# Latent and context convolved by one instruction per tap, and six heads' k and v handed to the delta rule's preparation in on-chip tiles

## Chip, core and metric

The kernel runs on one core of one Trainium2 chip. TensorE multiplies matrices, VectorE, ScalarE and GpSimd do the elementwise work, and SyncE (SP) issues the DMAs. The metric is the device time of one execution in microseconds (us), lower is better.

## The reference, cut to what matters

The program is a three-layer sequence model on 512 latent positions (8 rows of 64) and 256 context positions, width 2048. The change lies in the first layer. There the input is projected by `w_in`, and the projections go through a convolution over 5 neighbouring positions and a silu. In the latent part the convolution runs within rows of 64, in the context along all 256:

```python
xbc_l = jax.nn.silu(conv_latent(xbc_l, conv_ssd_w) + conv_ssd_b)
xbc_c = jax.nn.silu(centred_dwconv(xbc_c, conv_ssd_w) + conv_ssd_b)
qkv_l = jax.nn.silu(conv_latent(qkv_l, conv_gdn_w))
qkv_c = jax.nn.silu(centred_dwconv(qkv_c, conv_gdn_w))
ssd_c, ssd_l = ssd_mixer(xbc_c, dt_c, xbc_l, dt_l, ssd_a_log, ssd_dt_bias, ssd_d)
gdn_c, gdn_l = gdn_mixer(qkv_c, b_c, a_c, qkv_l, b_l, a_l, gdn_a_log, gdn_dt_bias)
```

`ssd_mixer` is a state-space scan over chunks of 128 positions in both directions. `gdn_mixer` is the delta rule: for each of 8 heads k is normalized, k kT of each chunk is decayed and masked, a unit lower triangular system is solved per chunk, and a scan in both directions follows. The two later layers use none of this.

## The kernel before, in words

Phase A of layer 1 works in channel-major form. One *block* is 128 output channels: a *gemm* accumulates `mm` (128 channels x 512 latent positions) and `mmc` (128 x 256 context positions) in PSUM over 16 slices of the width, with three products each, since weights and activations are split in a high part (`wh`, `hi`) and a low one (`wl`, `xlo`). L200 is the line of these products, L185 and L186 split the weights. Four PSUM buffers (pool `pm`) hold `mm` and `mmc`, so two blocks are in flight.

When a block's products are done, `conv5` convolves it. ScalarE copies PSUM into a padded tile (L438) and writes the middle tap, scaled (L440, with a bias L442); VectorE adds four more taps (L444); ScalarE takes a tanh (L446) and VectorE multiplies (L447), which together make the silu, as the taps are halved beforehand. Context (`cvc`) and latent part (`cvl`) each go through this on their own. 26 blocks have both parts, and four latent ones (two C blocks, q0, q1) have one.

Then a *sink* uses the result. For the SSD these are `xt`, `Bf`/`Bt` and `Cf`, read by `ssd_unit` (units 0 to 3, four heads each). A unit first runs backward (d=1): per chunk, state products `st`, the state `H` (L620, L622), the product `yo` of the state with C (L603), and `y` (L607). Then forward (d=0), where `ssd_diag` adds the part within a chunk: `Rf`/`Rb` (rows of the decay, by DMA), `Z` (L649), Z times exp (L652), `yd` (L655), and y's sum (L658 to L663). At the end `yT` transposes y, ScalarE copies it to `yf` (L629) and a DMA stores it to `yr`. For the delta rule, k and v of each head are stored to DRAM, `kD` and `vD` (L800, L801), and `gdn_prep(h)` loads them back as `kf` and `vf` (L670, L672), makes the decay E, transposes k and v, and stores ktD, vtD, ED, XD, LX. `gdn_solve` solves two heads' systems at a time, on GpSimd.

Heads 0 and 1's k and v are convolved between units 1 and 2, those of heads 2 to 7 between the preparations: k2, preparation 0, v2, preparation 1, k3, preparation 2, v3, and so on. The pool of the SSD units (`sp`) is released after unit 3, and the preparations' pool (`gp`) is opened on the same side of the memory, over it:

```python
            self.ssd_unit(u, self.xts[u])
        self.sp.release()
        self.b2 = tc.alloc_tile_pool(name="b2", bufs=1, side="right")
        with tc.tile_pool(name="gp", bufs=1, side="right") as self.gp:
            self.gemm([bk(2)])
            self.gdn_prep(0)
            self.gemm([bv(2)])
            self.gdn_prep(1)
```

The engines' queues in phase A are not in the order of the source. The framework's scheduler orders the whole block when the kernel is built, from its own estimates, and the pools limit what may be moved: a gemm's block stands where a PSUM tile is free by its reckoning. In before the gemms of k2 to v3 stand among unit 3's products. After phase A come q1 and the first gate block z0, and phase B, the scan with the other gate blocks z1 and on woven into it.

Of the kernel before, what the change touches and what calls it, by code (L numbers as in the profile page):

```python
# [9 lines left out]
F32 = mybir.dt.float32  # L10
F32R = mybir.dt.float32r
AF = mybir.ActivationFunctionType
# [3 lines left out]
P = 128  # L16
# [5 lines left out]
MUL, ADD, SUB, MAX, MIN = ALU.mult, ALU.add, ALU.subtract, ALU.max, ALU.min  # L22
# [111 lines left out]
class Prog:  # L134
# [278 lines left out]
        return self.hc[:, o:o + 1]  # L413

    def pads_lat(self, pool):
        self.pads(pool, 0)

    def pads(self, pool, nctx=2):
        nc = self.nc
        self.padl = [pool.tile([P, 8, 68], F32, name=f"padl{i}") for i in range(2)]  # L420
        self.padc = [pool.tile([P, 1, 260], F32, name=f"padc{i}") for i in range(nctx)]
        for p, n in [(p, 64) for p in self.padl] + [(p, 256) for p in self.padc]:
            nc.gpsimd.memset(p[:, :, 0:2], 0.0)
            nc.gpsimd.memset(p[:, :, n + 2:n + 4], 0.0)
        self.npl = self.npc = 0

    def conv5(self, ps, is_lat, taps, bias, out, th):

        nc = self.nc
        if is_lat:  # L430
            pad, n, r = self.padl[self.npl % len(self.padl)], 64, 8
            self.npl += 1
        else:
            pad, n, r = self.padc[self.npc % len(self.padc)], 256, 1
            self.npc += 1
        pv = ps.rearrange("p (r n) -> p r n", r=r)
        ov = out.rearrange("p (r n) -> p r n", r=r)
        nc.scalar.activation(out=pad[:, :, 2:n + 2], in_=pv, func=AF.Copy)  # L438
        if bias is None:
            nc.scalar.activation(out=out, in_=ps, func=AF.Identity, scale=taps[2])  # L440
        else:
            nc.scalar.activation(out=out, in_=ps, func=AF.Identity, scale=taps[2], bias=bias)  # L442
        for j in (0, 1, 3, 4):
            nc.vector.scalar_tensor_tensor(out=ov, in0=pad[:, :, j:j + n], scalar=taps[j], in1=ov,  # L444
                                           op0=MUL, op1=ADD)
        nc.scalar.activation(out=th, in_=out, func=AF.Tanh)  # L446
        nc.vector.scalar_tensor_tensor(out=out, in0=th, scalar=1.0, in1=out, op0=ADD, op1=MUL)  # L447

    def both(self, src, done, share=None):

# [7 lines left out]
                    acts=[(self.xh, self.xl, ps[:m, :], "l%d" % id(ps)),  # L458
                          (self.ch, self.cl, pc[:m, o:o + 256], "c%d" % id(pc))], done=done)

    def conv_block(self, names, j, has_bias, sink):

        taps = [self.h(names + str(i), j) for i in range(5)]
        bias = self.h("cb", j) if has_bias else None

        def done(ps, pc=None):
            outs = []
            for p, n, t in ((pc, 256, "c"), (ps, 512, "l")):
                if p is None:
                    outs.append(None)  # L470
                    continue
                o = self.cv.tile([P, n], F32, tag="cv" + t, name="cv" + t)
                th = self.cv.tile([P, 512], F32, tag="cth", name="cth", bufs=1)
                self.conv5(p, t == "l", taps, bias, o, th[:, :n])
                outs.append(o)
            sink(outs[1], outs[0])
        return done

    def small_done(self, ps, pc):
# [186 lines left out]
    def gdn_prep(self, h):  # L666
        nc, g = self.nc, self.gp
        v6 = lambda a: a.rearrange("p (c n) -> p c n", n=P)
        kf = g.tile([P, 768], F32, name="kf")
        nc.sync.dma_start(kf, self.kD[h])  # L670
        vf = g.tile([P, 768], F32, name="vf")
        nc.sync.dma_start(vf, self.vD[h])  # L672
        E = g.tile([P, 768], F32, name="E")
        Rb = g.tile([P, 768], F32, name="Rgb")
        nc.sync.dma_start(E, self.AA[64 + h].partition_broadcast(P))
# [1 line left out]
        for c in range(6):  # L677
            s = slice(c * P, (c + 1) * P)
# [14 lines left out]
        junk = g.tile([P, P], F32, name="junk", bufs=1)  # L693
        for c0, n in ((0, 4), (4, 2)):
            q = self.sc("kT")
            self.transposes(q, None, [kf[:, (c0 + i) * P:(c0 + i + 1) * P] for i in range(n)])
# [9 lines left out]
        for d in range(2):  # L706
            nc.vector.tensor_tensor(out=self.Dg[:, h, d], in0=self.beg[:, :, 8 * d + h], in1=rk2, op=MUL)
            nc.vector.tensor_tensor(out=self.DDE[:, h, d], in0=self.Dg[:, h, d],
                                    in1=self.DEg[:, :, 8 * d + h], op=MUL)

        vt = g.tile([P, 6, P], F32, name="vt")
        for c0, n in ((0, 4), (4, 2)):
            q = self.sc("vT")
            self.transposes(q, None, [vf[:, (c0 + i) * P:(c0 + i + 1) * P] for i in range(n)])
            nc.vector.tensor_tensor(out=vt[:, c0:c0 + n], in0=v6(q[:, :n * P]),
                                    in1=ss[:, c0:c0 + n].unsqueeze(2).to_broadcast([P, n, P]), op=MUL)
        nc.sync.dma_start(self.vtD[h], vt)
        masked(1, vf[:, 0:512], nc.gpsimd, self.mL)

        X = g.tile([P, 768], F32, name="X")  # L720
        for c0, n in ((0, 4), (4, 2)):
            q = self.sc("kk")
            for i in range(n):
                s = slice((c0 + i) * P, (c0 + i + 1) * P)
                nc.tensor.matmul(q[:, i * P:(i + 1) * P], kf[:, s], kf[:, s], start=True, stop=True)
# [6 lines left out]
        for b in range(4):  # L732
            r = slice(32 * b, 32 * b + 32)
# [34 lines left out]
    def phase_a(self):  # L768
        nc, tc, D = self.nc, self.tc, self.D
# [17 lines left out]
        self.xts = {}  # L787

        def sink_x(j):
            def f(lat, ctx):  # L790
# [78 lines left out]

    def query_conv(self, h, ps):  # L870
        o = self.b2.tile([P, 512], F32, name="qf", bufs=2)
        th = self.cv.tile([P, 512], F32, tag="cth", name="cth", bufs=1)
        self.conv5(ps, True, [self.h(f"cg{i}", h) for i in range(5)], None, o, th)
        self.qf.append(o)


# [1169 lines left out]
```

## Time and profile before

| | before |
|---|---|
| median of 3 runs | 3466.33 us (3462.2 to 3469.05) |
| profiled execution | 3458.53 us, span 3456.8 us |
| mean granted TensorE clock | 0.99 |
| TensorE busy | 3342.1 us (97%) |
| VectorE busy | 2084.7 us (60%) |
| ScalarE busy | 1448.1 us (42%) |
| GpSimd busy | 416.3 us (12%) |
| DMA | 482.04 MB, 139 GB/s over the span |

Busy shares are means over the whole span; phase A takes about a fifth of it, 0 to some 710 us, and the stretches in it are told apart by the windows. The clock is a share of full speed, 1.0 for 2.4 GHz and 0.5 for 1.2 GHz. The profiled execution is 7.8 us below the median of the runs.

### The profile page before, as it was taken

The page shows a single profiled execution, that of the slowest core. Times are in us where ns is not written, and L with a number is a line of the kernel's source. Part 1 is how long each engine was busy: PE and PEld are TensorE (multiplying, and loading weights), DVE is VectorE, ACT ScalarE, POOL GpSimd, SP SyncE. Part 2 cuts the span into 40 slices and gives each one's busy share as a digit, 9 for nine tenths or more (in the row PEclk, how much of TensorE's full clock was granted, in tenths as well). Part 3 has the DMA queues.
Part 4 walks back from the last instruction along what each step waited for, and adds up shares of the span by engine and source line. Part 5 has one row for each costly group of instructions (what it writes and reads, how often), then busy time and mean ns, then how long its engine had stood idle before and what let it go on. Part 6 is the DMA issues. An engine that isn't in the chain of part 4 may idle for free.

```text
span 3456.8 us, 47795 instructions
## 1 busy us (share of the span) xinstructions
PE 3342.1 (97%) x16950; PEld 2786.7 (81%) x16950; DVE 2084.7 (60%) x4117; ACT 1448.1 (42%) x2923; POOL 416.3 (12%) x596
## 2 busy tenths in 40 slices
PE   5999999899999999999999999999999999999998
PEld 4888888778888787778888788887888888878887
DVE  5678768778765647776747644555444444353456
ACT  4343335354444336664434444343333333342334
POOL 0011127821110000002313100000000000000000
PEclk8999999999999999999999999999999999999999
DMA  9533338555443854433333744543333333354345
GB/s 375 188 101 103 86 115 255 171 165 156 125 119 99 283 194 161 112 110 101 107 96 97 224 133 126 155 119 109 106 104 104 102 100 103 95 159 128 89 130 172
DMA packets 278350, 482.04 MB, mean 139 GB/s; under 512 B 51976, under 2 KB 85128, under 8 KB 273888
## 3 DMA queue, kind: packets, MB, share of 16 engines
q1 hardware_dynamic: 278112, 479.00, 46.8%
q8 instruction: 133, 2.18, 0.3%
q14 instruction: 105, 0.86, 0.1%
HBM read 417.53 MB, written 61.34 MB: 139 GB/s over the span
## 4 chain that ended last, share of the span: by engine, by line
PE 76%; DVE 9%; DMA 8%; POOL 2%; ACT 2%; issue 2%; SPq 0%; DVEq 0%; ACTq 0%; POOLq 0%
PE mm L200 57%; PE mm L228 3%; PE mm L230 3%; PE mm L232 3%; PE mmc L200 2%; DVE wl L186 2%; PE pl L200 1%; PE mg L930 1%; DMA Rf<-AA 1%; DMA araw<-yF 1%; PE pr L349 1%; DMA wa<-in_wada 1%; PE s L200 1%; DMA E<-AA 1%; POOL E L679 1%
## 5 line engine op out<-in xcount | busy, mean ns | idle before, releaser
L200 PE MATMUL mm<-hi,wl 128*128 128x512 f32 (+2 forms) x3632 | 1416.0, 391 | 15.9 <-DVE wl L186 10.3
L200 PE MATMUL mm<-xlo,wh 128*128 128x512 f32 (+2 forms) x3632 | 1420.8, 391 | 0.2
L200 PE MATMUL mm<-hi,wh 128*128 128x512 f32 (+2 forms) x3632 | 1414.9, 390 | 0.0
L186 DVE TENSOR_TENSOR wl<-wr,wh 128x512 fp32r<-128x512 f32 (+1 forms) x940 | 653.2, 700 | 647.8 <-ACT wh L185 644.9
L185 ACT ACTIVATE wh<-wr 128x512 fp32r<-128x512 f32 (+1 forms) x940 | 580.4, 621 | 1080.4 <-PE mm L200 860.3
L200 PEld LDWEIGHTS mm<-hi,wl 128*128 128x128 f32 (+1 forms) x3632 | 685.1, 189 | 141.6 <-DVE wl L186 14.8
L200 PEld LDWEIGHTS mm<-xlo,wh 128*128 128x128 f32 (+1 forms) x3632 | 685.1, 189 | 135.8 <-issue 2.9
L200 PEld LDWEIGHTS mm<-hi,wh 128*128 128x128 f32 (+1 forms) x3632 | 684.9, 189 | 120.0 <-issue 4.3
L232 PE MATMUL mm<-wh,hi 128*128 128x512 f32 x384 | 150.4, 392 | 0.0
L230 PE MATMUL mm<-wh,xlo 128*128 128x512 f32 x384 | 149.7, 390 | 0.0
L228 PE MATMUL mm<-wl,hi 128*128 128x512 f32 x384 | 149.7, 390 | 0.0
L223 DVE TENSOR_TENSOR wl<-wr,wh 128x512 fp32r<-128x512 f32 x96 | 69.7, 727 | 94.1 <-ACT wh L222 93.8
L222 ACT ACTIVATE wh<-wr 128x512 fp32r<-128x512 f32 x96 | 60.6, 631 | 152.3 <-PE mm L232 95.5
L200 PE MATMUL mmc<-xlo,wh 128*128 128x256 f32 x368 | 106.1, 288 | 0.0
L444 DVE SCALAR_TENSOR_TENSOR cvl<-padl,hc,cvl 128x512 f32<-128x512 f32 x112 | 90.2, 812 | 25.7 <-ACT cvl L440 15.6
L200 PE MATMUL mmc<-hi,wl 128*128 128x256 f32 x368 | 105.6, 287 | 0.0
L200 PE MATMUL mmc<-hi,wh 128*128 128x256 f32 x368 | 105.5, 287 | 0.0
L228 PEld LDWEIGHTS mm<-wl,hi 128*128 128x128 f32 x384 | 72.1, 188 | 15.0 <-DVE pad L1360 0.3
L230 PEld LDWEIGHTS mm<-wh,xlo 128*128 128x128 f32 x384 | 72.1, 188 | 15.0
L232 PEld LDWEIGHTS mm<-wh,hi 128*128 128x128 f32 x384 | 72.1, 188 | 14.5
L200 PEld LDWEIGHTS mmc<-xlo,wh 128*128 128x128 f32 x368 | 70.0, 190 | 15.7
L200 PEld LDWEIGHTS mmc<-hi,wh 128*128 128x128 f32 x368 | 69.9, 190 | 15.1
(585 smaller groups left out, 3992.2 us busy)
## 6 DMA issues: line engine op xcount, KB each, us to landing
wr<-in_o_in SPq DMA_DIRECT2D x192, 256.0 KB, 3.1
wr<-in_e_in SPq DMA_DIRECT2D x160, 256.0 KB, 3.1
wr<-in_pgate SPq DMA_DIRECT2D x148, 256.0 KB, 3.4
wa<-in_wada SPq DMA_DIRECT2D x16, 2048.0 KB, 10.4
wr<-in_w_qkv SPq DMA_DIRECT2D x96, 256.0 KB, 3.4
wr<-in_w_z SPq DMA_DIRECT2D x64, 256.0 KB, 3.2
wr<-in_w_out SPq DMA_DIRECT2D x64, 256.0 KB, 3.7
wg<-in_wgate SPq DMA_DIRECT2D x16, 1024.0 KB, 7.2
```

Source lines behind the costliest of these rows:

```text
L185: nc.scalar.activation(out=hi, in_=r, func=AF.Copy)
L186: nc.vector.tensor_tensor(out=lo, in0=r, in1=hi.bitcast(F32), op=SUB)
L200: nc.tensor.matmul(ap, w[:, kk, :], x, start=(n == 0), stop=(n == total[key] - 1))
L222: nc.scalar.activation(out=hi, in_=r, func=AF.Copy)
L223: nc.vector.tensor_tensor(out=lo, in0=r, in1=hi.bitcast(F32), op=SUB)
L228: nc.tensor.matmul(ps[c][:, :n], self.xh[k][:, t], lo[:, i], start=first, stop=False)
L230: nc.tensor.matmul(ps[c][:, :n], self.xl[k][:, t], hi[:, i], start=False, stop=False)
L232: nc.tensor.matmul(ps[c][:, :n], self.xh[k][:, t], hi[:, i], start=False, stop=last)
L349: nc.tensor.matmul(pr[32 * j:32 * j + 32, 0:256], c32[:, 4 * q + j, :], w[:, 4 * q + j, :], start=(q == 0), stop=(q == 3), tile_position=( ...
L444: nc.vector.scalar_tensor_tensor(out=ov, in0=pad[:, :, j:j + n], scalar=taps[j], in1=ov, op0=MUL, op1=ADD)
L679: nc.gpsimd.tensor_scalar(out=E[:, s], in0=E[:, s], scalar1=self.AAg[:, c, h:h + 1], scalar2=None, op0=SUB)
L930: nc.tensor.matmul(v[:, c], lhs[:, c], rhs[:, c], start=True, stop=True)
```

## The change

`conv5` takes both parts at once. One padded tile of 12 rows x 68 holds the 8 latent rows and the context as 4 rows of 64, whose margins hold the neighbouring context values; two copies of 3 rows x 66 out of PSUM, at offsets 0 and 62, fill these rows with their margins. Each tap, the tanh and the final multiply are then one instruction on 768 columns. The tanh is written into the padded tile, and the tile `cth` is gone. The results lie in one tile of 768, latent first.

For heads 2 to 7 this tile is a `kv` tile of the pool `gp`, of which there are six, and `gdn_prep` reads k and v from it. Their v is no longer stored to DRAM, k still is (the scan loads it later). Heads 0 and 1 are stored and loaded as before, with two loads each. GpSimd's masked E, which was written over vf, has a tile of its own, `Em`.

```diff
     def pads_lat(self, pool):
-        self.pads(pool, 0)
-
-    def pads(self, pool, nctx=2):
+        self.pads(pool, 8)
+
+    def pads(self, pool, rows=12):
         nc = self.nc
-        self.padl = [pool.tile([P, 8, 68], F32, name=f"padl{i}") for i in range(2)]
-        self.padc = [pool.tile([P, 1, 260], F32, name=f"padc{i}") for i in range(nctx)]
...
+        self.pad = [pool.tile([P, rows, 68], F32, name=f"pad{i}") for i in range(2)]
...
-    def conv5(self, ps, is_lat, taps, bias, out, th):
+    def conv5(self, ps, pc, taps, bias, out):
...
-        nc.scalar.activation(out=pad[:, :, 2:n + 2], in_=pv, func=AF.Copy)
-        if bias is None:
-            nc.scalar.activation(out=out, in_=ps, func=AF.Identity, scale=taps[2])
...
+        nc.scalar.activation(out=pad[:, 0:8, 2:66], in_=ps.rearrange("p (r n) -> p r n", r=8), func=AF.Copy)
+        parts = [(ps, out[:, 0:512])]
+        rows = 8
+        if pc is not None:
+            rows = 12
+
+            w = lambda o: bass.AP(tensor=pc.tensor, offset=pc.offset + o, ap=[list(pc.ap[0]), [64, 3], [1, 66]])
+            nc.scalar.activation(out=pad[:, 8:11, 2:68], in_=w(0), func=AF.Copy)
+            nc.scalar.activation(out=pad[:, 9:12, 0:66], in_=w(62), func=AF.Copy)
+            parts.append((pc, out[:, 512:768]))
+        for p, o in parts:
+            if bias is None:
+                nc.scalar.activation(out=o, in_=p, func=AF.Identity, scale=taps[2])
...
+        ov = out.rearrange("p (r n) -> p r n", r=rows)
         for j in (0, 1, 3, 4):
-            nc.vector.scalar_tensor_tensor(out=ov, in0=pad[:, :, j:j + n], scalar=taps[j], in1=ov,
+            nc.vector.scalar_tensor_tensor(out=ov, in0=pad[:, 0:rows, j:j + 64], scalar=taps[j], in1=ov,
                                            op0=MUL, op1=ADD)
-        nc.scalar.activation(out=th, in_=out, func=AF.Tanh)
-        nc.vector.scalar_tensor_tensor(out=out, in0=th, scalar=1.0, in1=out, op0=ADD, op1=MUL)
+
+        th = pad[:, 0:rows, 2:66]
+        nc.scalar.activation(out=th, in_=ov, func=AF.Tanh)
+        nc.vector.scalar_tensor_tensor(out=ov, in0=th, scalar=1.0, in1=ov, op0=ADD, op1=MUL)
...
-    def conv_block(self, names, j, has_bias, sink):
+    def conv_block(self, names, j, has_bias, sink, keep=False):
...
+            n = 512 if pc is None else 768
+            o = (self.gp.tile([P, 768], F32, tag="kv", name="kv", bufs=6) if keep else
+                 self.cv.tile([P, 768], F32, tag="cv", name="cv"))[:, :n]
+            self.conv5(ps, pc, taps, bias, o)
+            sink(o[:, 0:512], None if pc is None else o[:, 512:768])
...
     def gdn_prep(self, h):
-        kf = g.tile([P, 768], F32, name="kf")
-        nc.sync.dma_start(kf, self.kD[h])
-        vf = g.tile([P, 768], F32, name="vf")
-        nc.sync.dma_start(vf, self.vD[h])
+        def chunks(dst):
+            lat, ctx = self.kv.pop((id(dst), h), (None, None))
+            if lat is None:
+                t = g.tile([P, 768], F32, tag="kv", name="kv", bufs=6)
+                lat, ctx = t[:, 0:512], t[:, 512:768]
+                nc.sync.dma_start(lat, dst[h, :, 256:768])
+                nc.sync.dma_start(ctx, dst[h, :, 0:256])
+            return [ctx[:, 0:P], ctx[:, P:2 * P]] + [lat[:, c * P:(c + 1) * P] for c in range(4)]
+
+        kf, vf = chunks(self.kD), chunks(self.vD)
...
-        masked(1, vf[:, 0:512], nc.gpsimd, self.mL)
+        masked(1, g.tile([P, 512], F32, name="Em"), nc.gpsimd, self.mL)
...
         def sink_kv(dst, h):
             def f(lat, ctx):
-                nc.sync.dma_start(dst[h, :, 256:768], lat)
-                nc.sync.dma_start(dst[h, :, 0:256], ctx)
+                if h > 1:
+                    self.kv[id(dst), h] = lat, ctx
+                if h < 2 or dst is self.kD:
+                    nc.sync.dma_start(dst[h, :, 256:768], lat)
+                    nc.sync.dma_start(dst[h, :, 0:256], ctx)
             return f
...
-        bk = lambda h: self.both(K(h), cb("cg", 8 + h, False, sink_kv(self.kD, h)))
-        bv = lambda h: self.both(V(h), cb("cg", 16 + h, False, sink_kv(self.vD, h)))
+        bk = lambda h: self.both(K(h), cb("cg", 8 + h, False, sink_kv(self.kD, h), h > 1))
+        bv = lambda h: self.both(V(h), cb("cg", 16 + h, False, sink_kv(self.vD, h), h > 1))
```

Lines behind conv5 have other numbers in the changed kernel: L446 is the scaled copy there (L440 before), L607 and L619 are yo and st (L603 and L615), L633 is yf (L629), L659 is yd (L655).

In the order of TensorE before, this is the place where k3 (mm_5012, mmc_5013) ends and v3 (mm_5246, mmc_5247) begins; yo, yd and st are unit 3's.

```order
L200 MATMUL mm_5012<-hi_910,wh_5106 128x512
L200 MATMUL mmc_5013<-xlo_918,wh_5106 128x256
L200 MATMUL mmc_5013<-hi_917,wh_5106 128x256
L200 MATMUL mm_5246<-hi_295,wl_5251 128x512
L603 MATMUL yo_4283<-H_4280,Cf_3353 128x256
L655 MATMUL yd_4308<-xt_4058,Z_4289 128x64 x4
L615 MATMUL st_4322<-xd_4320,Bt_3259 128x256
L200 MATMUL mmc_5247<-hi_302,wl_5251 128x256
L200 MATMUL mm_5246<-xlo_296,wh_5250 128x512
```

In the changed kernel TensorE's order has this at the end of v2 (mm_4586, mmc_4587):

```order
L200 MATMUL mm_4586<-hi_910,wh_4680 128x512
L200 MATMUL mmc_4587<-xlo_918,wh_4680 128x256
L200 MATMUL mmc_4587<-hi_917,wh_4680 128x256
L619 MATMUL st_4114<-xd_4112,Bt_3174 128x256
L607 MATMUL yo_4119<-H_4116,Cf_3267 128x256
L619 MATMUL st_4124<-xd_4122,Bt_3174 128x256
L607 MATMUL yo_4129<-H_4126,Cf_3267 128x256
L619 MATMUL st_4134<-xd_4132,Bt_3174 128x256
L607 MATMUL yo_4139<-H_4136,Cf_3267 128x256
L619 MATMUL st_4144<-xd_4142,Bt_3174 128x256
```

and this at the end of unit 3, 15 rows on, where k3 (mm_4882) begins:

```order
L619 MATMUL st_4292<-xd_4290,Bt_3174 128x256
L607 MATMUL yo_4297<-H_4294,Cf_3267 128x256
L659 MATMUL yd_4322<-xt_3948,Z_4303 128x64 x4
L314 MATMUL yT_4334<-ident_78,y_4103 128x128 x3
L314 MATMUL yT_4342<-ident_78,y_4103 128x128 x3
L314 MATMUL yT_4334<-ident_78,y_4103 128x128
L314 MATMUL yT_4342<-ident_78,y_4103 128x128
L200 MATMUL mm_4882<-hi_295,wl_4887 128x512
L200 MATMUL mm_4882<-xlo_296,wh_4886 128x512
```

Between v2's last product and k3's first there are 25 rows, all of unit 3; before, gemm products stand among them.

ScalarE in the changed kernel, at the end of unit 3: `kv_4479` is k2's tile and `kv_4708` that of v2, both written from their PSUM tiles.

```order
L650 ACTIVATE Z_4303<-cbL_3270,dts_1482 128x128 x4
L633 ACTIVATE yf_4339<-yT_4334 128x512
L633 ACTIVATE yf_4347<-yT_4342 128x512
L446 ACTIVATE kv_4479<-mm_4357,hc_93 128x512
L446 ACTIVATE kv_4479<-mmc_4358,hc_93 128x256
L446 ACTIVATE kv_4708<-mm_4586,hc_93 128x512
L446 ACTIVATE kv_4708<-mmc_4587,hc_93 128x256
L455 ACTIVATE pad0_928<-kv_4479 128x12x64
```

The scaled copies of k2 and v2 stand behind both yf copies; before, the scaled copies of k2, v2 and k3 stand ahead of these.

SP's queue before, at the preparation of head 7 (`vD_942`, `ktD_944` and so on are its stores), up to the branch that ends phase A's block:

```order
L801 DMA vD_942<-cvc_6949 128x256
L800 DMA vD_942<-cvl_6959 128x512
L672 DMA vf_7056<-vD_942 128x768
L701 DMA ktD_944<-kt_7077 128x768
L766 DMA LT_948<-T_5768 96x1024
L717 DMA vtD_945<-vt_7105 128x768
L687 DMA ED_943<-vf_7056 128x512
L728 DMA XD_946<-X_7119 128x768
```

and the same place in the changed kernel:

```order
L700 DMA ED_939<-Rgb_6819 128x512
L700 DMA ED_939<-Em_6877 128x512
L182 DMA wr_7024<-in_w_z 128x512
L182 DMA wr_7042<-in_w_z 128x512
L714 DMA ktD_940<-kt_6837 128x768
L730 DMA vtD_941<-vt_6865 128x768
L740 DMA XD_942<-X_6880 128x768
```

The store and load of v7 are gone, and both masked E are stored ahead of ktD.

## Rows read from the trace of the kernel before

**Rows 1.** Windows: stretch, length, busy PE PEld DVE ACT POOL, clock, DMA, GB/s
```profile
148.00:441.00 293.00, 289.06 (x1670) 252.65 (x1669) 235.96 (x544) 128.69 (x284) 37.92 (x46) 1.00 0.37 99
441.00:449.00 8.00, 4.58 (x15) 3.70 (x14) 6.59 (x12) 1.72 (x4) 3.12 (x4) 0.67 0.41 114
449.00:703.00 254.00, 238.04 (x1365) 207.58 (x1363) 189.05 (x372) 107.87 (x292) 156.98 (x226) 0.98 0.61 188
703.00:760.00 57.00, 50.31 (x248) 42.03 (x247) 40.57 (x90) 25.28 (x54) 9.24 (x12) 0.91 0.60 173
```

**Rows 2.** Waits of PE, 520 to 700: total us, times, longest
```profile
PE vT L314 <- DMA vf<-vD: 10.5, 4, 5.3
PE kT L314 <- DVE Xs L738: 2.7, 1, 2.7
PE vT L314 <- DVE cvl L444: 1.7, 1, 1.7
PE kT L314 <- DMA kf<-kD: 1.0, 1, 1.0
```

**Rows 3.** Instructions of source line L444: ns min/median/max
```profile
L444 DVE SCALAR_TENSOR_TENSOR cvl<-padl,hc,cvl x112: 734/745/1300, 147.3 to 676.2; 128x512 f32<-128x512 f32 x112
L444 DVE SCALAR_TENSOR_TENSOR cvc<-padc,hc,cvc x104: 440/477/1896, 151.8 to 678.8; 128x256 f32<-128x256 f32 x104
```

**Rows 4.** Lines by form, ACT, 140 to 720: busy us, mean ns
```profile
L438 ACT ACTIVATE padc<-mmc 128x256 f32<-128x256 f32 x23 | 8.8, 383 | 0.0
```

**Rows 5.** Timeline of DVE, and between them the chain, 426 to 448
```profile
427.24 0.41 DVE L663 TENSOR_TENSOR y<-yt,yd 128x256 f32<-128x256 f32 x1
...
431.08 4.92 DMA Rf<-AA
...
444.49 0.42 DVE L622 TENSOR_TENSOR H<-H,st 128x256 f32<-128x256 f32 x1
```

**Rows 6.** Timeline of PE and DVE, one backward step: start us, us
```profile
458.62 0.59 PE L603 MATMUL yo<-H,Cf 128*128 128x256 f32 x2
...
459.26 0.42 DVE L607 TENSOR_TENSOR y<-yo,EAs 128x256 f32<-128x256 f32 x1 [1.28 <-PE yo L603]
459.69 0.42 DVE L622 TENSOR_TENSOR H<-H,st 128x256 f32<-128x256 f32 x1
```

**Rows 7.** Lines by form, DVE, 140 to 720: busy us, mean ns
```profile
L649 DVE SCALAR_TENSOR_TENSOR Z<-cbU,dts,Z 128x128 f32<-128x128 f32 x64 | 22.3, 384 | 0.0
...
L652 DVE TENSOR_TENSOR Z<-Z,Rf 128x512 f32<-128x512 f32 x16 | 10.8, 680 | 0.0
```

**Rows 8.** Chain that ended last, 480 to 512: start us, us, what
```profile
484.22 0.43 PE yo L603 x2
484.65 0.84 PE yd L655 x8
...
495.89 0.61 ACT yf L629
496.51 3.44 DMA yr<-yf
...
500.66 2.16 DMA yr<-yf
```

**Rows 9.** Windows of two stretches, columns as in Rows 1
```profile
25.00:50.00 25.00, 9.95 (x78) 5.54 (x79) 16.30 (x26) 15.04 (x29) 0.00 (x0) 0.61 1.01 391
441.00:444.50 3.50, 0.64 (x4) 0.38 (x2) 3.40 (x6) 0.56 (x2) 2.51 (x3) 0.88 0.42 128
444.50:449.00 4.50, 3.94 (x11) 3.32 (x12) 3.19 (x7) 1.16 (x3) 0.62 (x1) 0.50 0.41 104
```

**Rows 10.** Timeline of SP, and tile vf's transfers: us to landing
```profile
682.34 0.33 SPq L800 DMA_DIRECT2D vD<-cvl  x1
...
698.56 2.59 SPq L182 DMA_DIRECT2D wr<-in_w_z  x4
...
DMA to landing us min/median/max: 2.0/3.3/6.8
```

More of the change, by code (lines that the diff above doesn't have):

```diff
@@ L415, in pads_lat @@
     def pads_lat(self, pool):
-        self.pads(pool, 0)
-    def pads(self, pool, nctx=2):
+        self.pads(pool, 8)
+    def pads(self, pool, rows=12):
         nc = self.nc
-        self.padl = [pool.tile([P, 8, 68], F32, name=f"padl{i}") for i in range(2)]
-        self.padc = [pool.tile([P, 1, 260], F32, name=f"padc{i}") for i in range(nctx)]
[L422 to L425, printed above, removed]
@@ L427, in conv5 @@
-    def conv5(self, ps, is_lat, taps, bias, out, th):
-        nc = self.nc
[L430 to L437, printed above, removed]
-        nc.scalar.activation(out=pad[:, :, 2:n + 2], in_=pv, func=AF.Copy)
-        if bias is None:
-            nc.scalar.activation(out=out, in_=ps, func=AF.Identity, scale=taps[2])
-        else:
-            nc.scalar.activation(out=out, in_=ps, func=AF.Identity, scale=taps[2], bias=bias)
+        self.pad = [pool.tile([P, rows, 68], F32, name=f"pad{i}") for i in range(2)]
@@ new lines, in pads @@
+        for p in self.pad:
+            nc.gpsimd.memset(p[:, 0:min(rows, 9), 0:2], 0.0)
+            nc.gpsimd.memset(p[:, 0:8, 66:68], 0.0)
+            if rows > 8:
+                nc.gpsimd.memset(p[:, 11, 66:68], 0.0)
+        self.np = 0
+    def conv5(self, ps, pc, taps, bias, out):
+        nc = self.nc
+        pad = self.pad[self.np % 2]
+        self.np += 1
+        nc.scalar.activation(out=pad[:, 0:8, 2:66], in_=ps.rearrange("p (r n) -> p r n", r=8), func=AF.Copy)
[10 more added lines that the diff above has]
+                nc.scalar.activation(out=o, in_=p, func=AF.Identity, scale=taps[2])
+            else:
+                nc.scalar.activation(out=o, in_=p, func=AF.Identity, scale=taps[2], bias=bias)
+        ov = out.rearrange("p (r n) -> p r n", r=rows)
@@ L466, in done @@
         def done(ps, pc=None):
[L467 to L476, printed above, removed]
+            n = 512 if pc is None else 768
[3 more added lines that the diff above has]
+            sink(o[:, 0:512], None if pc is None else o[:, 512:768])
         return done
@@ L668, in gdn_prep @@
         v6 = lambda a: a.rearrange("p (c n) -> p c n", n=P)
-        kf = g.tile([P, 768], F32, name="kf")
-        nc.sync.dma_start(kf, self.kD[h])
-        vf = g.tile([P, 768], F32, name="vf")
-        nc.sync.dma_start(vf, self.vD[h])
+        nc, g = self.nc, self.gp
+        v6 = lambda a: a.rearrange("p (c n) -> p c n", n=P)
+        def chunks(dst):
[7 more added lines that the diff above has]
+        kf, vf = chunks(self.kD), chunks(self.vD)
         E = g.tile([P, 768], F32, name="E")
@@ L695, in gdn_prep @@
             q = self.sc("kT")
-            self.transposes(q, None, [kf[:, (c0 + i) * P:(c0 + i + 1) * P] for i in range(n)])
+            self.transposes(q, None, kf[c0:c0 + n])
             nc.scalar.activation(out=kt[:, c0:c0 + n], in_=v6(q[:, :n * P]), func=AF.Copy)
@@ L713, in gdn_prep @@
             q = self.sc("vT")
-            self.transposes(q, None, [vf[:, (c0 + i) * P:(c0 + i + 1) * P] for i in range(n)])
+            self.transposes(q, None, vf[c0:c0 + n])
             nc.vector.tensor_tensor(out=vt[:, c0:c0 + n], in0=v6(q[:, :n * P]),
@@ L723, in gdn_prep @@
             for i in range(n):
-                s = slice((c0 + i) * P, (c0 + i + 1) * P)
-                nc.tensor.matmul(q[:, i * P:(i + 1) * P], kf[:, s], kf[:, s], start=True, stop=True)
+                nc.tensor.matmul(q[:, i * P:(i + 1) * P], kf[c0 + i], kf[c0 + i], start=True, stop=True)
             nc.vector.tensor_tensor(out=X[:, c0 * P:(c0 + n) * P], in0=q[:, :n * P],
@@ L786, in phase_a @@
         K, V = (lambda h: D["w_qkv"][8 + h]), (lambda h: D["w_qkv"][16 + h])
-        self.xts = {}
+        self.xts, self.kv = {}, {}
         def sink_x(j):
@@ L871, in query_conv @@
         o = self.b2.tile([P, 512], F32, name="qf", bufs=2)
-        th = self.cv.tile([P, 512], F32, tag="cth", name="cth", bufs=1)
-        self.conv5(ps, True, [self.h(f"cg{i}", h) for i in range(5)], None, o, th)
+        self.conv5(ps, None, [self.h(f"cg{i}", h) for i in range(5)], None, o)
         self.qf.append(o)
```

## Prediction

> **What bounds the kernel now.** I read the windows by stage first, because the edits touch only the first part of the kernel, 148 to about 703 us, and its hand-over to the scan [rows 1]. TensorE carries this part. From 148 to 441 us it is busy 289.06 of 293.00 us, at granted clock 1.00, while VectorE is busy 235.96 and ScalarE 128.69. So whatever is saved on VectorE there can move the end by no more than TensorE's own idle time, 293.00 − 289.06 = 3.9 us. The next two windows are worse: 441 to 449 us has 4.58 busy of 8.00 at clock 0.67, and 449 to 703 has 238.04 of 254.00 at 0.98. The window after the hand-over, 703 to 760, has 50.31 of 57.00 at 0.91.
>
> Next I asked what TensorE waits for between 520 and 700 us, the delta rule's preparation [rows 2]. The four rows give 15.9 us, all of that window's idle time: 10.5 us in four waits of the vT transposes for the reloaded vf, 1.0 us of kT for the reloaded kf, 2.7 us for Xs (an earlier preparation on VectorE) and 1.7 us for a convolution that was just being finished. The first two, 11.5 us, are the round trip through DRAM that the change removes for six heads.
>
> **Merged convolution.** A tap on 512 columns takes 745 ns, one on 256 takes 477 [rows 3]. The 256 columns more cost 268 ns, so I put 768 columns at 745 + 268 = 1013 ns (an estimate from these two rows). A tap pair falls from 1222 to 1013 ns, 209 ns less, and the final multiply, of the same widths, by about as much: 5 × 209 ns × 26 blocks = 27 us of VectorE work. Its worth goes by the windows: at most 3.9 us up to 441, and I take 0, because the order of TensorE's work decides there. If VectorE did decide there it would be the 3.9. On ScalarE the context's one pad copy becomes two, about one more of 383 ns [rows 4], and two tanh become one; ScalarE has over half of 148 to 441 free, so I take nothing. Were it not hidden, 26 × 383 ns = 10 us would be the outside cost.
>
> **No reload.** Twelve stores of v, and twelve loads of k and v, leave SP's queue. On the path this is worth the 11.5 us of [rows 2], between 520 and 700 us. What remains there is 2.7 + 1.7 = 4.4 us of other waits, and some 1.6 us of clock: call it 6. Bounds: 2, if the merged taps also take the convolution's and Xs's waits away, and 9.5, which is before's whole loss in the window (16.0 idle + 238.04 × 0.02 = 4.8 of clock, 21 in all) less the 11.5.
>
> **What the order moves: unit 3 stands alone.** This is the term that decides. The kv tiles lie in the memory of the SSD units' pool, which is released only after unit 3. So ScalarE cannot write the scaled copy of k2 or v2 into kv before unit 3's last store has read its yf; those two heads' four PSUM tiles are all that there are, and k3's first product waits. On TensorE, k2 and v2 run ahead of unit 3, and then its 25 rows stand without one product of a gemm beside them. In before, the gemms k2 to v3 ran between these rows and filled their waits. How long is the chain, from v2's last product to k3's first?
>
> (a) Until unit 3's first H is there. In before, unit 2's last y began at 427.24, and H's sum (L622) at 444.49 [rows 5], 17.3 us later, with the load of Rf in between, issued at 431.08 and landed 4.92 us later. Some 2 us of taps that stood between no longer do: 15. In the changed order 46 products stand between unit 2's last transpose and v2's end, which at 289.06 us for 1670 of them [rows 1] are 8 us: 15 − 8 = 7. Bounds 4 and 11.
> (b) The backward direction, four steps. One step is yo at 458.62, y at 459.26, H's sum at 459.69, which takes 0.42 [rows 6], and 0.14 until the next product: 1.63 us. Four are 6.5.
> (c) The forward direction is VectorE's: between its first H and its last y stand 20 operations of 0.42, eight Z of 0.384, two products of Z and exp at 0.68 [rows 7] and three xd of about 0.5: 8.4 + 3.1 + 1.4 + 1.5 = 14.4 us. Bounds 12 and 18 (waits for TensorE in each of four chunks).
> (d) The tail: one transpose 0.2, yf 0.61, its store 3.44, the second yf as long as the first (yf has one buffer, so it waits for that store), its store 2.16 [rows 8], and the scaled copy of k2 of about 0.7: with the steps between, 8. Bounds 6.4 and 9.4.
> (e) Six products of 0.43 lie on this path. At half clock they take twice as long: 2.6.
>
> The sum is 7 + 6.5 + 14.4 + 8 + 2.6 = 38.5 us, with bounds of about 29 and 47. Unit 3's own products in it are worth 17 × 0.43 + 4 × 0.84 (yd, [rows 8]) + 0.9 for the transposes = 11.5 us; the other 27 us TensorE stands still.
>
> Half clock is what the rows show after thin stretches: 0.61 from 25 to 50 us, where TensorE is busy 9.95 of 25 us, and 0.50 from 444.5 to 449, right after 3.5 us in which it did 0.64 [rows 9]. So I take the lower level (1.2 GHz) for unit 3 and for as long behind it as those 4.5 us: 2.2 us more. The Trainium skill, "TensorE: Matmul & The Clock Gate", section "HAM oscillation — how this bites in real kernels", speaks against this change in the same way: work in bursts with waits between them makes the clock fall, and each next burst starts cold. By that rule the 2.6 and 2.2 are due, as I have them; without it the sum would be 4.8 us less.
>
> **The sum up to z0's end.** At full clock the products from 441 to 703 are worth 2.5 (0.64 × 0.88 + 3.94 × 0.50) + 233 (254 − 21) = 235.5 us, in both kernels. Without unit 3's 11.5 that is 224. Changed kernel: 441 + 224 + 38.5 + 2.2 + 6 = 711.7 against 703: 8.7 us later.
>
> **The hand-over.** In before, the last preparation stores v7 at 682.34 and reloads it (from issue to landing this tile's transfers take 2.0 us at the shortest, 3.3 in the median), and its chain ends in X, whose reload stands ahead of the gate weights of z1 in SP's queue (698.56) [rows 10]. Store and reload are gone: at least 2.0 + 3.3 = 5.3 us earlier relative to z0. The window 703 to 760 loses 6.7 us of idle time [rows 1], so 0 to 6.7 can come back; I take 5. Later stages read the same data in the same order: 0.
>
> Net 8.7 − 5 = +3.7 us. The profiled execution took 3458.53 us, so the changed one should take about 3462; the median of before stands 7.8 above its profiled one, and I put the changed median at 3466.3 + 3.7 = 3470.
>
> **Rivals.** A measurement here tells about 0.2%, 7 us, from no change.
> - *Unit 3's chain is longer (slower).* If H comes 10 us after v2's end, and both yr stores take 3.44, and the forward direction waits for TensorE, the chain is about 46 us: 46 − 38.5 = 7.5 more, so +11, 3478. It decides from a chain of about 42 us on. For it: every figure of (a) to (d) comes from rows in which work was at hand, and the loads of Rf share SP's queue with weights. Against it: VectorE has no convolution to do meanwhile. Chance 0.36.
> - *The chain is shorter, and the reloads were worth more (faster).* A chain of 30 us with full clock, and 3 us left of the waits: 8.5 + 3 less, so −8, 3458; with more given back at the hand-over, 3455. For it: the waits for vf also delayed the next blocks' drains. Chance 0.20.
> - *VectorE's 27 us show in the time (faster).* Then 3440 to 3450. Against it: TensorE's 3.9 us of idle time before 441. Chance 0.04.
> - *Forecast, within 0.2%* (3459.4 to 3473.3): 0.40.
>
> Faster by over 0.2% 0.24, within 0.40, slower 0.36. The chain's bounds alone are −9 and +9 around 3470, those of the remaining waits −4 and +3.5, of the hand-over +5 and −2; taken together I put the range at 3456 to 3485.
>
> **What would show it.** Right: on TensorE a gap of gemm products of some 35 to 42 us that begins near 441, with a granted clock near 0.5 to 0.7; VectorE's tap on 768 columns at about 1013 ns; no vT wait for a DMA after 520; z0's last product near 712, and less idle time in the 57 us after it. Wrong: k3's first product well before 475 or after 490; or new waits in the preparations, of VectorE for GpSimd's ss (its queue holds the solve), or of vT for the kv taps, which would put the waits left over 10 us.

## The result, and the profile after

The changed kernel takes 3486.37 us in the median of 6 runs (3478.51 to 3494.99), the kernel before 3461.09 (3458.42 to 3469.05, 6 runs). The ratio is 1.008, interval 1.0065 to 1.0096: some 25 us slower, and just above the forecast's range of 3456 to 3485. The profiled execution took 3481.38 us (span 3479.7), 22.9 us of span more than before.

The windows of the changed kernel, columns as in [rows 1]. The first stretch answers to the first there; the others are unit 3, the restart behind it, the preparations up to z0's end, and the start of the scan:

```profile
148.00:441.00 293.00, 289.07 (x1671) 252.30 (x1670) 225.49 (x460) 129.47 (x280) 40.40 (x43) 1.00 0.35 96
...
444.60:487.00 42.40, 25.42 (x76) 18.01 (x74) 22.29 (x56) 8.44 (x21) 7.55 (x11) 0.57 0.12 34
487.00:491.00 4.00, 4.00 (x10) 3.13 (x11) 3.64 (x4) 1.23 (x3) 0.00 (x0) 0.50 0.83 269
491.00:734.50 243.50, 227.74 (x1288) 198.57 (x1286) 167.15 (x280) 102.93 (x279) 161.62 (x220) 0.96 0.55 165
734.50:792.00 57.50, 52.25 (x276) 43.36 (x275) 42.02 (x95) 27.43 (x57) 8.09 (x10) 0.97 0.55 156
```

Up to 441 us TensorE did the same as before, 289.07 us, with VectorE 10 us less busy: nothing was gained there. Then the clock falls to 0.57 for 42 us, and in the 243.5 us up to z0's end 15.8 us are idle and, at clock 0.96, another 0.04 × 227.74 = 9.1 us are lost. The hand-over window loses 5.2 us instead of 6.7, at clock 0.97 instead of 0.91.

TensorE's waits between 500 and 735 us (us in total, times, longest), which answer to [rows 2]:

```profile
PE vT L314 <- DVE kv L456: 15.2, 4, 7.1
PE kT L314 <- DVE vt L728: 0.4, 1, 0.4
PE vT L314 <- DVE X L738: 0.2, 1, 0.2
```

No wait for DRAM is left. But the transposes of v now wait 15.2 us for the tap chain's last multiply (L456) on the tile itself; before, all waits of that stage were 15.9. Two windows of the changed kernel around the second of these waits, which lasts until 595.4, show what such a wait costs besides:

```profile
589.80:595.40 5.60, 2.09 (x15) 1.85 (x14) 5.23 (x7) 3.12 (x7) 5.16 (x6) 0.83 0.40 127
595.40:600.00 4.60, 4.60 (x16) 3.92 (x16) 3.42 (x5) 3.38 (x17) 4.18 (x6) 0.50 0.02 6
```

The products behind it run at half clock (0.50) for 4.6 us, and at 0.73 and 0.68 behind the first and the third.

The merged tap (L451; min/median/max ns), which answers to [rows 3]:

```profile
L451 DVE SCALAR_TENSOR_TENSOR cv<-pad,hc,cv x64: 735/1010/1490, 154.8 to 407.0; 128x768 f32<-128x768 f32 x56, 128x512 f32<-128x512 f32 x8
L451 DVE SCALAR_TENSOR_TENSOR kv<-pad,hc,kv x48: 1001/1019/2649, 487.3 to 707.7; 128x768 f32<-128x768 f32 x48
```

The medians are close to the forecast's 1013 ns. Single long taps are not new: in the kernel before, a tap of 256 columns reached 1896 ns against a median of 477 [rows 3].

Unit 3, from the chain that ended last (start us, us, what), with TensorE's timeline at both ends:

```profile
444.33 0.28 PE L200 MATMUL mmc<-hi,wh 128*128 128x256 f32 x1
...
441.46 4.53 DMA Rf<-AA
...
451.33 1.19 PE yo L607 x2
452.52 0.87 PE st L619 x2
453.42 0.43 DVE H L626
...
453.98 1.19 PE yo L607 x2
...
462.89 0.43 DVE H L626
...
467.72 1.22 PE yo L607 x2
468.94 1.60 PE yd L659 x8
470.54 0.97 PE st L619 x2
471.54 0.43 DVE H L626
...
479.12 1.51 PE yT L314 x7
480.65 0.61 ACT yf L633
481.28 1.99 DMA yr<-yf
483.37 0.61 ACT yf L633
483.99 2.01 DMA yr<-yf
...
486.98 0.80 PE L200 MATMUL mm<-hi,wl 128*128 128x512 f32 x1 [6.15 <-ACT kv L446]
```

v2's last product starts at 444.33, k3's first at 486.98, released by the copy of k2 into its kv tile: 42.65 us without a gemm. The first yo stands 7.0 us behind v2's end, as forecast. One backward step takes 453.98 − 451.33 = 2.65 us, since yo (1.19) and st (0.87) both lie on the path and both run at half clock [rows 6, 8].

In the forward direction too the path is TensorE's: of the 4.25 us from yo's start at 467.72 to the end of H's sum, 3.79 are yo, yd and st. How long this takes goes with the clock. `e19_late`, described below, runs the same chain, but there the clock rose to full inside it. The forward direction of the changed kernel, and then that of `e19_late`:

```profile
462.90:479.60 16.70, 14.63 (x50) 11.75 (x51) 11.35 (x30) 2.55 (x8) 4.34 (x6) 0.50 0.00 0
462.10:475.20 13.10, 8.28 (x53) 6.63 (x53) 11.79 (x30) 2.56 (x8) 4.40 (x6) 1.00 0.00 0
```

At full clock the direction takes 13.1 us, VectorE is busy for 11.79 of them, and the whole gap is 38.57 us (38.43 in `e7_Edve`, whose clock rose as well). In the five kernels with six kept heads and the merged convolution whose clock over the chain was 0.53 to 0.57, the gap was 41.4 to 43.5 us. What lets the clock rise in two of them is open: up to the forward direction TensorE was busy 9.53 us in the changed kernel and in `e19_late` alike.

VectorE's waits for GpSimd from 440 to 735 us, of the changed kernel:

```profile
DVE vt L728 <- POOL ss L718: 25.6, 5, 10.5
DVE E L694 <- POOL E L692: 15.5, 8, 5.5
```

and of the kernel before:

```profile
DVE E L681 <- POOL E L679: 8.3, 6, 2.1
...
DVE vt L715 <- POOL ss L705: 4.9, 3, 3.4
```

Here ss is k's norm per position, a power on 128x6. From the end of the sum that it reads to its own start it stood 9.75, 15.60 and 12.58 us in three heads of the changed kernel, with 11, 17 and 17 rows of the solve ahead of it; in the kernel before, where it stood longest, 7.56, 4.77 and 9.93 us, with 2, 5 and 11 rows. So it was late before, too; VectorE then waited for it 3.4 us at the longest, and 10.5 in the changed kernel. Part of the longest delay is GpSimd's own wait for a load of the solve:

```profile
609.95 0.16 POOL L767 MEMSET T<- 96x32 f32 x1 [7.34 <-DMA T<-LX]
...
614.93 1.35 POOL L718 TENSOR_TENSOR ss<-ss,half 128x6 f32<-128x6 f32 x1
```

What this does to VectorE's queue is seen in its timeline around the longest of the vT waits (start us, us, instruction, idle time before it and what ended it):

```profile
616.31 1.02 DVE L728 TENSOR_TENSOR vt<-vT,ss 128x512 f32<-128x512 f32 x2 [10.46 <-POOL ss L718]
...
625.29 3.61 DVE L694 SCALAR_TENSOR_TENSOR E<-Rgb,AAg,E 128x128 f32<-128x128 f32 x6 [3.19 <-DMA LX<-Xt]
...
630.54 4.00 DVE L451 SCALAR_TENSOR_TENSOR kv<-pad,hc,kv 128x768 f32<-128x768 f32 x2
...
639.25 1.39 DVE L456 SCALAR_TENSOR_TENSOR kv<-pad,kv 128x768 f32<-128x768 f32 x1
```

VectorE ran these in the order of its queue. It stood 10.46 us for ss, then 3.19 us for a DMA ahead of E, and only then came v5's taps, two of which took 4.00 us beside GpSimd's solve and its masked E. The tile was ready at 640.6 us; the products of v5 had ended at 615.8.

### The profile page after: what moved, and what is told of

Read it like the earlier page. It is cut to its first block, busy times and chain, and to the rows that moved or that the text cites. A ratio compares the mean times of both kernels' runs of the same rounds, so it can differ in the third digit from the quotient of the medians.

```text
span 3479.7 us, 47610 instructions
## 1 busy us (share of the span) xinstructions
PE 3352.2 (96%) x16950; PEld 2791.5 (80%) x16950; DVE 2067.4 (59%) x3987; ACT 1448.8 (42%) x2923; POOL 427.7 (12%) x594
## 4 chain that ended last, share of the span: by engine, by line
PE 78%; DVE 7%; DMA 6%; POOL 4%; ACT 2%; issue 2%; SPq 0%; DVEq 0%; POOLq 0%; ACTq 0%
PE mm L200 59%; PE mm L228 3%; PE mm L232 3%; PE mm L230 3%; PE mmc L200 2%; POOL To L772 1%; POOL T L774 1%; DVE wl L186 1%; PE pl L200 1%; PE pr L349 1%; PE mg L944 1%; DMA Rf<-AA 1%; PE s L200 1%; DMA araw<-yF 1%; PE lv L1624 1%
## 5 line engine op out<-in xcount | busy, mean ns | idle before, releaser
L200 PEld LDWEIGHTS mmc<-xlo,wh 128*128 128x128 f32 x368 | 69.7, 189 | 15.9
L200 PEld LDWEIGHTS mmc<-hi,wh 128*128 128x128 f32 x368 | 69.7, 189 | 15.2
```

The lines of the kernel that those rows point to most:

```text
L200: nc.tensor.matmul(ap, w[:, kk, :], x, start=(n == 0), stop=(n == total[key] - 1))
```

## The experiments

Times are medians; each ratio is to runs of the kernel before on the same chip. Not all groups of runs are from one chip, so kernels of different groups are compared by their ratios. The first four take the change apart.

**The convolution alone** (`e1_conv`): the kernel before with the new `conv5`; `kf` and `vf` as before.

```diff
-            sink(outs[1], outs[0])
+            self.conv5(ps, pc, taps, bias, o)
+            sink(o[:, 0:512], None if pc is None else o[:, 512:768])
```

> The kernel before with the merged convolution alone; k and v of all heads go through DRAM as before. Theory A (the loss comes from where the kv tiles lie, so that unit 3 stands alone on TensorE): no gap near 444 us, and 3450 to 3465 us against some 3461 for before. Rival B (the merged taps themselves make the convolution end later, and that is what TensorE waits for): some 15 us of vT waits between 520 and 700, and 3470 us or more.

3476.35 us, ratio 1.0045 (1.003 to 1.0059). No gap at 444, yet slower. TensorE's waits from 440 to 735 us begin with

```profile
PE mm L200 <- DVE wl L186: 15.9, 1, 15.9
PE vT L314 <- DMA vf<-vD: 13.1, 5, 10.3
PE kT L314 <- DMA kf<-kD: 7.3, 5, 3.1
```

and SP's timeline has, at the hand-over,

```profile
714.95 0.33 SPq L770 DMA_DIRECT2D LT<-T  x1
715.32 0.43 SPq L966 DMA_DIRECT2D X<-XD  x1
...
718.91 2.08 SPq L182 DMA_DIRECT2D wr<-in_w_z  x4
```

The store of the second solve's result comes at 714.95 us (688.58 before), and behind it in SP's queue stand X's reload and z1's weights [rows 10], for which TensorE waited 15.9 us. Neither theory had this; the vT waits that rival B expected are there, but for the reload and not for the taps. In the new order unit 3's stores come at 502.45 instead of 496.51, the preparations and with them the solves start later, and GpSimd ends 26 us later.

**The kv tiles alone** (`e2_kv`): latent and context convolved apart, in the same tile.

```diff
-            self.conv5(ps, pc, taps, bias, o)
+            for p, t, l in ([] if pc is None else [(pc, o[:, 512:768], False)]) + [(ps, o[:, 0:512], True)]:
+                self.conv5(p, l, taps, bias, t)
```

> The changed kernel with latent and context convolved apart again, in the same kv tile; the six heads' k and v stay on chip. Theory A: the gap without gemm products between v2 and k3 is there, 40 to 45 us, and the time is 3478 to 3492 us. Rival B: gap and loss are smaller, 3470 us or less, since the taps are as before.

3472.4 us, 1.004 (1.0025 to 1.0055). The gap is there, 22 rows of unit 3 from 444.3 to 474.9 us: 30.6 us, shorter than expected; the time lies between the two theories. 12.7 us of vT waits for the kv tile are there too, though the taps are the old ones. So neither half is harmless alone: 17 and 13 us, and 25 together.

**Fewer heads kept** (`e3_h3`, `e4_h4`): head 2, or heads 2 and 3, through DRAM.

```diff
-                if h > 1:
+                if h > 3:
...
-                if h < 2 or dst is self.kD:
+                if h < 4 or dst is self.kD:
```

> The changed kernel, but head 2 too is stored and reloaded, so that k2 and v2 are drained into the convolutions' pool while unit 3 runs. Theory A: TensorE's gap of 42.7 us goes and its 27 us of idle time and 4 to 5 us of half clock with it: 3450 to 3460 us. Rival C (the gap only moves: k3 and v3 then wait for unit 3's memory): a gap of 20 us or more before k4, 3470 to 3480 us.

> The changed kernel, but heads 2 and 3 are stored and reloaded, four heads are kept. Theory A: no gap at unit 3, 3448 to 3460 us; the vT waits for DRAM come back for two heads at most. Rival C: as with one head, the time stays above 3470 us.

With one head fewer: 3478.81 us, 1.006 (1.0045 to 1.0075). The gap moved, as rival C said, though it is smaller and has another end: k3 and v3 now run beside unit 3, and behind them TensorE waits for a preparation's reload of k into a kv tile:

```profile
502.92 1.51 PE L314 MATMUL kT<-ident,kv 128*128 128x128 f32 x6 [8.88 <-DMA kv<-kD]
...
506.51 0.78 PE L200 MATMUL mm<-hi,wl 128*128 128x512 f32 x1
```

k4 begins 15.6 us after v3's last product (490.9), and the vT waits for kv tiles are 17.0 us. With two heads fewer the gap is gone, and 441 to 449 us is 8.00 busy of 8.00: 3472.97 us, 1.0038 (1.0025 to 1.0051). So the kv memory does cause the gap, but without it the kernel is still 13 us slower than before. In the four-head kernel 11.7 us of one vT wait for a kv tile stay, and 8.1 us for gate weights.

**GpSimd out of VectorE's way.** The next runs move the first subtraction of E to VectorE, and make ss there by a multiplication, which leaves its square root out.

```diff
-            nc.gpsimd.tensor_scalar(out=E[:, s], in0=E[:, s], scalar1=self.AAg[:, c, h:h + 1],
+            nc.vector.tensor_scalar(out=E[:, s], in0=E[:, s], scalar1=self.AAg[:, c, h:h + 1],
...
-        nc.gpsimd.tensor_tensor(out=ss, in0=ss, in1=self.half6, op=ALU.pow)
+        nc.vector.tensor_tensor(out=ss, in0=ss, in1=self.half6, op=MUL)
```

The subtraction alone, on the changed kernel, on the kernel before, and on the convolution alone; and the second solve called four heads later (`if h == 7`):

> The changed kernel, with the first subtraction of the decay E (48 instructions of some 0.6 us) on VectorE instead of GpSimd. Unit 3 still stands alone, and the gap of some 43 us at 444 stays. Theory D (what is lost behind unit 3 is GpSimd: E stands in its queue between the solve's instructions, VectorE waits for E, and the last v's taps stand behind E): the vT waits for the kv tile, 15.2 us in the changed kernel, fall under 6, and the time falls by some 10 us to about 3473 to 3477. Rival F (the transposes of v simply stand too close behind v's products in TensorE's order): vT waits of 12 us or more stay, 3482 us or more.

> The kernel before with the same subtraction on VectorE. A control: theory D expects little, 3455 to 3465 us, because there the preparations waited for DRAM; if it gains 10 us or more, the subtraction's place is worth as much without the change, and the run of the changed kernel says nothing about the change.

> The kernel before with the merged convolution alone (3476 us), and the subtraction on VectorE. Theory D: the second solve ends earlier than the 713 us at which it holds back the next gate block's weights, z1's first product comes without a wait of over 5 us, and the time is 3455 to 3465 us. Rival F: the waits stay, 3472 us or more.

> The changed kernel with the second solve called behind head 7's preparation instead of head 3's, so that GpSimd has only one solve to mix with the preparations of heads 4 to 7. Theory D: the vT waits before 735 fall from 15.2 to 8 us or less, but the solve ends later and may hold the scan of heads 2 and 3: 3470 to 3485 us. Rival F: the vT waits stay at 12 us or more.

- `e7_Edve` 3490.24, 1.0072 (1.0055 to 1.0089): vT waits 15.9 us, no gain; VectorE still waits 19.0 us for ss.
- `e9_before_Edve` 3464.69, 1.001 (0.9996 to 1.0023): the control moves little.
- `e10_conv_Edve` 3464.27, 1.0004 (0.9994 to 1.0013), against 3476.35 without the edit: the second solve's store comes at 679.64 and the wait at z1 falls from 15.9 to 1.2 us. GpSimd's late end was the loss of the merged convolution alone. And with it gone, the merged convolution gains nothing against its control; the waits for reloads are 22.2 us there, as against 11.5 before.
- `e5_solve7` 3491.19, 1.0073 (1.0056 to 1.009): inconclusive. The scheduler put the solve where it was (611 to 668 us, as against 610 to 667), so the edit did not do what it was for.

ss alone, both on the changed kernel, both on the kernel before, both with four heads kept:

> The changed kernel, with ss made on VectorE by a multiplication with the same tile of halves instead of the power on GpSimd: the square root is left out. Theory S (VectorE's vt stands in its queue waiting for GpSimd's ss, which stands behind up to 28 rows of the solve: 25.6 us in the changed kernel, 4.9 before; all that is queued behind vt, the next v's taps too, is late): VectorE's wait for ss goes, the vT waits of TensorE fall from 15.2 us to 8 or less, 3470 to 3480 us. Rival F (the transposes of v stand too close behind v's products, whatever GpSimd does): vT waits of 12 us or more stay, 3483 us or more.

> The changed kernel with both ss (the multiplication, square root left out) and the first subtraction of E on VectorE, so that VectorE waits for GpSimd in the preparations no more. Theory S: vT waits 5 us or less, unit 3's gap of some 43 us stays, 3464 to 3474 us. Rival F: 3480 us or more.

> The kernel before with both ss (the multiplication, square root left out) and the first subtraction of E on VectorE. A control: theory S expects 3452 to 3463 us, since VectorE waited for GpSimd only 13 us there and TensorE waited for DRAM.

> The changed kernel with four heads kept instead of six (no gap at unit 3), and both ss (the multiplication, square root left out) and the first subtraction of E on VectorE. If unit 3's place and GpSimd's queue are the whole loss, this is faster than the kernel before: 3440 to 3454 us, with no wait over 3 us for a kv tile. Rival F: 3462 us or more.

- `e12_ss` 3498.69, 1.0111 (1.0096 to 1.0126): VectorE waits 40.2 us for GpSimd's E instead, up to 15.4 at once, and the vT waits are 20.4. The time is longer, not shorter.
- `e13_ssE` 3483.48, 1.007 (1.0055 to 1.0085): VectorE waits for GpSimd no more. TensorE's waits from 490 to 735 us are then

```profile
PE vT L314 <- DVE kv L456: 7.3, 2, 6.1
PE kk L737 <- ACT junk L712: 4.2, 1, 4.2
PE mm L200 <- DVE wl L186: 0.9, 1, 0.9
```

 Together 12.4 us, instead of 15.8. VectorE now stands for E's load, 20.2 us (8 waits, longest 9.0) between 440 and 735 us. Theory S was right about the wait and wrong about its worth.
- `e14_before_ssE` 3462.48, 1.0004 (0.9993 to 1.0016): the control, unmoved.
- `e17_h4_ssE` 3464.77, 1.0014 (1.0004 to 1.0024): without the gap, and with both operations on VectorE, it is by the ratios 8 us better than four heads alone, still not better than before; 10.2 us of vT waits remain. Of the 0.8% by which the changed kernel is slower, 0.14% are left.

**The transposes of v later.** In the changed order 17.3 us of products (one block, k of the next head) stand between v's last product and its transposes for heads 3 to 6, by the products' own durations; before it was 64, 45, 25 and 18 us.

```diff
-                self.gdn_prep(h)
                 if h < 7:
                     self.gemm([bv(h + 1)])
+                self.gdn_prep(h)
```

> The changed kernel with each preparation called behind the next head's v instead of its k, so that one more block of products stands between v's last product and its transposes (36 us of products instead of 17 for heads 3 to 6). Unit 3 still stands alone. Theory F (v's convolution is ready only 22 to 26 us after its products, since VectorE's queue holds waits ahead of its taps, and the order allows 17): vT waits fall from 15.2 us to 4 or less, 3470 to 3477 us. Rival G (what VectorE waits for only moves: the next block's PSUM is drained as late as the transposes were): TensorE waits 10 us or more for the kv copy instead, 3482 us or more.

> The same order with four heads kept instead of six, so without the gap at unit 3. Theory F: vT waits 4 us or less, 3450 to 3460 us, about as fast as before or faster. Rival G: 3468 us or more.

> The kernel before with each preparation called behind the next head's v. A control: its vT and kT waits for DRAM, 11.5 us, fall to 3 or less, and if the hand-over to the scan isn't later, 3447 to 3458 us; then the later call is worth as much without the change.

> The kernel before with the merged convolution, and each preparation called behind the next head's v. Theory F: the waits for DRAM (20 us in the merged convolution alone) fall to 4 or less, and the time from 3476 to 3450 to 3462 us, if the second solve doesn't again hold the gate weights at the hand-over; if it does, 3465 us or more.

- `e19_late` 3485.3, 1.0073 (1.0054 to 1.0092). TensorE's waits from 490 to 735 us:

```profile
PE kk L737 <- ACT junk L712: 7.0, 2, 5.2
PE mmc L200 <- ACT kv L446: 4.6, 1, 4.6
PE mm L200 <- DVE wl L186: 3.4, 2, 3.2
```

 The wait for the kv tile is gone, and as much has come back as waits for ScalarE's norms of k, for the copy that drains PSUM into kv, and for weights: rival G.
- `e20_h4_late` 3479.83, 1.0059 (1.0037 to 1.008): no better than four heads without it; kT waits 11.2 us for vt.
- `e22_before_late` 3461.07, 1.0004 (0.999 to 1.0018): the waits for DRAM fall from 11.5 to 9.5 us only, and 6.4 us come at the hand-over.
- `e23_conv_late` 3478.32, 1.0053 (1.0032 to 1.0074): the waits for DRAM are still 18.5 us, and 13.3 us of waiting at z1 are there again, with the second solve's store at 710.21.

**Everything together**: late transposes with both waits for GpSimd removed, six heads; and four heads, with ss's square root on ScalarE (`nc.scalar.activation(out=ss, in_=ss, func=AF.Sqrt)`).

> The changed kernel with the preparations one block later, and ss (a multiplication, square root left out) and the first subtraction of E on VectorE. Theory S+F (VectorE is late because it waits for GpSimd, and the transposes stand close behind): from k3's first product to z0's last some 232 us instead of 247, 3466 to 3474 us, the rest being unit 3's gap. Rival G (VectorE and ScalarE are late by their own queues): 240 us or more, 3480 us or more.

> Four heads kept, preparations one block later, the first subtraction of E on VectorE and the square root of ss on ScalarE. Theory S+F: no gap at unit 3 and no wait over 4 us in the preparations, 3448 to 3458 us, unless the changes of ScalarE's function table cost as much; rival G: 3464 us or more.

3490.21, 1.0089 (1.0072 to 1.0105), and 3473.65, 1.0036 (1.0024 to 1.0048). From k3's first product to z0's last the first takes 243.1 us, with 13.2 us of waiting for ScalarE's norms of k: rival G again. The second waits 12.0 us for ScalarE's norms, where 16 more table loads stand, and 7.6 us for z1's weights. No version beat the kernel before.

## Why the prediction was wrong

The forecast was 8.7 us later at z0's end. In the profiled execution z0's last product starts at 734.43 instead of 703.0, 31.4 us later. The forecast's own 711.7 misses it by 22.7, in two places: 4.1 in unit 3's chain and some 18.6 in the preparations behind it. The forecast time was 3.7 us on a median of 3466.3 for the kernel before; six runs put that median at 3461.1, so the forecast of the change itself was off by 21.6 us (25.3 measured).

- *What bounds the kernel* was right: VectorE's saving, 10 of the 27 us by 441, gave nothing up to there, and on its own it never showed in the time (`e10_conv_Edve` against its control).
- *Unit 3 stands alone* was right as a mechanism (`e4_h4` removes the gap, `e3_h3` moves it). Its size was off by 4.1 us, 42.65 against 38.5 and inside the bounds of 29 and 47. The start (a) was 7.0 as forecast, but by luck: from unit 2's last y (433.13) to H's sum (450.77) it is 17.6 us and not 15, and v2's last product begins 11.2 us behind that y and not 8. The backward direction took 11.6 against 6.5, the forward direction 16.7 against 14.4, and 2.6 of half clock were to come on top of both; the tail took 7.4 against 8. Half clock was priced on six products, but yo and st lie on the path in every backward step, and yo, yd and st in the forward chunks. So "The forward direction is VectorE's" was wrong at the clock that the prediction itself assumed; it fits `e19_late`, where the clock had risen.
- *Half clock* was right for this execution: 0.57 over the chain, 0.50 for 4 us behind it. The rule of the Trainium skill that the prediction weighed ("TensorE: Matmul & The Clock Gate", section "HAM oscillation — how this bites in real kernels") agrees with this fall. But the same chain also ran at 0.78 (`e19_late`).
- *No reload* is the step that failed: "what remains there is 2.7 + 1.7 = 4.4 us of other waits, and some 1.6 us of clock: call it 6", with bounds of 2 and 9.5. The rows give 15.8 us of idle time and 9.1 of clock between 491 and 734.5, and 2.0 of clock in the 4 us ahead of that: 26.9 us lost behind unit 3, where the sum had 2.2 + 6 = 8.2. The sum's 1.6 of clock has no row of its own; before lost 4.8 there. I took the reload's waits off and left everything else where it was. But TensorE's order is written from estimated times. With the store and load out of the path the transposes stand 17.3 us behind the products (64, 45, 25 and 18 before), and the tile was ready 25 us behind them (v5). The wait for DRAM became a wait for VectorE of the same size, 15.2 us, and behind its three longer pieces TensorE's clock was 0.73, 0.50 and 0.68. The place of the transposes is not the whole cause either: moved one block later (`e19_late`) they wait no more, and the stage from k3's first product to z0's last took 242.0 us instead of 247.5. Both waits that came, "of VectorE for GpSimd's ss (its queue holds the solve), or of vT for the kv taps", I had named as signs of being wrong, without a price or a chance.
- *The hand-over* was sized right by its window (4 us less lost, idle and clock together, for 5 forecast), but z1's first product comes only 2.2 us nearer to z0.
- The rival that the chain is longer was the right direction; but its mechanism was not the one that decided: 4.1 us more of chain would have made 3474. Of the 31.4 us, 2.2 came back at the hand-over and some 6 behind it in this execution; the runs' medians differ by 25.

The gap and GpSimd's two operations make up most of the loss when both are taken away (`e17_h4_ssE`, 1.0014, with two heads' reload back and no square root). Open is what sets the pace of the preparations with six heads. Each wait that was taken away (the kv tile, ss, E on GpSimd) left another one, for E's load, for the norms of k, for PSUM; from k3's first product to z0's last it was 247.5 us in the changed kernel, 240.9 with both waits for GpSimd gone (`e13_ssE`) and 243.1 with the late transposes as well (`e25_late_ssE`); the sum had 232. That these are all one chain per head, with single buffers, is an argument; no run showed it.

## What to carry to other kernels

When a scheduler writes the order from estimates, removing a transfer does not remove its wait: the consumer moves forward by what the scheduler believes, and waits for the next thing that it misjudges. Price the new producer's real lateness, with every engine that its queue stands behind, before the old wait is taken off. And ask of a new buffer what memory it lies over: tiles laid over a pool that is still in use left a chain alone on TensorE, whose waits gemm products had filled before. Price such a chain at both clocks, since at the lower one another engine may carry it: here the forward direction took 16.7 us at half clock, on TensorE's products, and 13.1 at full clock, on VectorE.

## What the runs showed of the hardware

VectorE's taps grew beside GpSimd's work. Between 480 and 700 us in the changed kernel, the 13 taps that ran with GpSimd idle for nine tenths of their time or more took 1017 ns in the median (longest 1021), the 31 others 1162 (mean 1279, longest 2649). The four longest up to 708 us (2046, 2047, 2610 and 2649 ns) all lay beside GpSimd's masked E, one instruction on 128x512. GpSimd's subtraction of E, 602 ns in the median, reached 1509. The Trainium skill, "GPSIMD Engine Reference", section "8. Key points", says that GpSimd shares its SBUF interfaces with VectorE, with contention where VectorE reads two tensors from SBUF, as a tap does. The long taps agree; but some taps wholly beside GpSimd's work did not grow (1018 ns at 491.17).

TensorE's granted clock over one and the same chain of small products was 0.57 in the changed kernel and 0.78 in `e19_late`, and the chain's gap 42.65 and 38.57 us.
